# A two-layer decoder step in float32: the FFN's first products as seven half-size products, the second product as a phase of its own

## The chip, the core and the metric

The kernel runs on one core of one Trainium2 chip. TensorE (PE) multiplies, VectorE (DVE) and ScalarE (ACT) do the elementwise work, SyncE (SP) issues nearly all DMAs from one queue, in order. The metric is device time in microseconds: for before, the median of three runs.

## The reference, cut to what matters

One step of a two-layer model for 1,024 prompt tokens and 32 sample tokens, which the kernel handles as 1,056 columns side by side. Layer 0 mixes with gated linear attention, layer 1 with dilated attention. After each mixer stands the same feed-forward network (FFN), with 1,024 features and a hidden width of 2,816:

```python
def swiglu_ffn(x, g, w_in, w_out):
    a, b = jnp.split(rms_norm(x, g) @ w_in, 2, axis=-1)
    return (jax.nn.silu(a) * b) @ w_out
...
        x = x + h.astype(x.dtype)
        x = x + swiglu_ffn(x, f_norm[i], f_w_in[i], f_w_out[i]).astype(x.dtype)
        x = x + per_layer_embed(x, p[i], e_norm[i], e_w_proj[i], e_w_gate[i]).astype(x.dtype)
```

`w_in` has 5,632 output columns: 22 tiles of 128 for `a` and 22 for `b`. All is float32.

## The kernel before

Features lie on the 128 partitions, tokens along the free axis: the residual stream is eight tiles `X[0..7]` of 128x1056. A product in nearly full precision is made of three matmuls in the type fp32r. Each operand is split into a high part (ACT's copy into fp32r) and a low part (DVE's subtraction of the high part), and hi·hi, hi·lo and lo·hi are added up in PSUM. `split` does this for tokens (`XH`, `XL`, `GH`, `GL`), and `wtile` for a weight tile of 128 output columns, which it loads first (`raw`, then `whi`, `wlo`).

`proj` multiplies one weight tile with all tokens: per tile of 128 input features three products, each in three matmuls of 352 columns (`CW`), so 72 matmuls where there are eight tiles of features. The two PSUM pools `mma` and `mmb` take turns, each of three banks.

`block` runs once per layer, and is what the change rewrites. The output projection of the mixer goes in two halves of the features (`mix_out`, or the end of `mixer` for the first half in layer 1). As the second half adds to `X[m]`, `second` renormalizes this tile into `XH[m]`, `XL[m]` (the gain alone; the factor 1/rms of a token, `rstd`, is applied to the product later) and adds its squares to `ssq`. `norm_done` sums `ssq` over the partitions with small matmuls (`p_n`) and takes a root on ACT and a reciprocal on DVE in three pieces.

The FFN then runs over the hidden tiles in five chunks (`FCH`). For each hidden tile two projections with `w_fi` give `a` and `b`, and `silu(a)*b` is split into `GH`, `GL`. After a chunk, eight products with `w_fo`, one for each `X[m]`, add the chunk's share to the residual. First and second products so alternate, and everything between them stays in SBUF.

The order within each engine comes from a scheduler in the build: it interleaves instructions of different phases, but each engine and each queue then runs strictly in that order. SP's queue holds the weight loads as well as the stores and loads of activations: an entry that waits holds up all behind it.

## Time and profile before

| | |
|---|---|
| median of three runs | 3043.79 us (3042.93 to 3048.19) |
| span of the profiled execution, first to last instruction | 3039.0 us |
| PE busy / PE weight loads busy | 2997.8 us (99%) / 2874.2 us (95%) |
| DVE busy / ACT busy | 1468.7 us (48%) / 956.5 us (31%) |
| matmuls, each with a weight load of its own | 18,900 |
| share of the chain that ended last: PE | 91%, of it line 164 (`proj`) 73% |

The span is the kernel's own part of a run; the runs shown lie 3.9 to 9.2 us above it. "PE busy" counts any time in which at least one matmul is in flight, and matmuls overlap: the mean duration of one is longer than the distance between the starts of two.

### The profile page before, as it was taken

The numbers are of one execution on the slowest core, as the hardware profiler recorded it, in microseconds if no ns is written. First come the engines' busy times: TensorE is split into PE (matmuls) and PEld (weight loads), VectorE is DVE, ScalarE is ACT, GpSimd is POOL, SyncE is SP. The second block draws the span as 40 slices with busy tenths as digits, with TensorE's granted clock in tenths as the row PEclk, the third lists the DMA queues.
The fourth block names the chain that finished last, engine by engine and source line by source line (L and its number), as shares of the span: only waits on it lengthen the run. The fifth ranks groups of instructions, "written<-read, shape, count | busy, mean of one in ns | idle before, by whom it ended". The sixth has DMA issues, their size and how long they took to land.

```text
span 3039.0 us, 43739 instructions
## 1 busy us (share of the span) xinstructions
PE 2997.8 (99%) x18900; PEld 2874.2 (95%) x18900; DVE 1468.7 (48%) x2095; ACT 956.5 (31%) x1515; POOL 20.1 (1%) x44
## 2 busy tenths in 40 slices
...
GB/s 131 54 71 50 72 126 102 42 42 51 38 58 35 57 46 60 28 78 90 141 97 104 51 120 43 113 125 113 59 36 55 37 54 43 42 52 60 32 62 76
DMA packets 109776, 208.65 MB, mean 69 GB/s; under 512 B 31472, under 2 KB 54000, under 8 KB 108560
## 3 DMA queue, kind: packets, MB, share of 16 engines
...
## 4 chain that ended last, share of the span: by engine, by line
PE 91%; DVE 4%; DMA 3%; ACT 1%; issue 1%; SPq 0%; ACTq 0%
PE mm L164 73%; PE mm L712 6%; PE mm L182 1%; PE p_s L759 1%; PE p_o L827 1%; DMA vv<-in_cv_dram 1%; DVE q L586 1%; DVE hs L594 1%; DMA kk<-in_ck_dram 1%; DVE q L596 1%; DVE hs L595 1%; PE p_u L390 1%; PE p_us L408 1%; PE p_s L748 1%; PE p_o L399 1%
## 5 line engine op out<-in xcount | busy, mean ns | idle before, releaser
L164 PE MATMUL mm<-XH,whi 128*128 128x352 f32 x3312 | 728.5, 326 | 2.1 <-ACT whi L120 2.1
L164 PE MATMUL mm<-XL,whi 128*128 128x352 f32 x3312 | 723.5, 325 | 0.0
L120 ACT CAST whi<-raw 128x1024 fp32r<-128x1024 f32 (+4 forms) x288 | 247.5, 859 | 1507.4 <-PE mm L164 1430.9
L164 PE MATMUL mm<-XH,wlo 128*128 128x352 f32 x3312 | 716.9, 324 | 0.0
L164 PEld LDWEIGHTS mm<-XH,whi 128*128 128x128 f32 x3312 | 563.9, 188 | 11.3 <-issue 3.1
L164 PEld LDWEIGHTS mm<-XH,wlo 128*128 128x128 f32 x3312 | 566.1, 189 | 2.3 <-issue 1.6
L164 PEld LDWEIGHTS mm<-XL,whi 128*128 128x128 f32 x3312 | 564.1, 188 | 3.1 <-issue 1.6
L121 DVE TENSOR_TENSOR wlo<-raw,whi 128x1024 fp32r<-128x1024 f32 (+4 forms) x288 | 282.0, 979 | 15.5 <-ACT whi L120 15.2
L164 PE MATMUL mm<-GL,whi 128*128 128x352 f32 x1302 | 279.3, 322 | 0.0
L164 PE MATMUL mm<-GH,wlo 128*128 128x352 f32 x1302 | 279.2, 322 | 0.0
L164 PE MATMUL mm<-GH,whi 128*128 128x352 f32 x1302 | 278.5, 322 | 0.0
L537 DVE TENSOR_TENSOR X<-mm,X 128x1056 f32<-128x1056 f32 (+1 forms) x84 | 101.0, 1204 | 301.2 <-PE mm L164 301.0
L532 DVE TENSOR_TENSOR s<-mm,s 128x1056 f32<-128x1056 f32 x44 | 55.4, 1258 | 344.2 <-PE mm L164 344.2
L164 PEld LDWEIGHTS mm<-GL,whi 128*128 128x128 f32 x1302 | 220.9, 188 | 0.5 <-DVE GL L121 0.5
L164 PEld LDWEIGHTS mm<-GH,wlo 128*128 128x128 f32 x1302 | 220.8, 188 | 0.0
L164 PEld LDWEIGHTS mm<-GH,whi 128*128 128x128 f32 x1302 | 220.8, 188 | 0.0
L191 DVE TENSOR_TENSOR s<-mm,rstd 128x1056 f32<-128x1056 f32 x42 | 52.8, 1258 | 342.1 <-PE mm L164 342.1
L712 PE MATMUL mm<-XL,whi 128*128 128x352 f32 x576 | 193.5, 336 | 0.0
L712 PE MATMUL mm<-XH,whi 128*128 128x352 f32 x576 | 192.7, 334 | 0.0
L712 PE MATMUL mm<-XH,wlo 128*128 128x352 f32 x576 | 189.3, 329 | 0.0
L712 PEld LDWEIGHTS mm<-XH,whi 128*128 128x128 f32 x576 | 108.5, 188 | 3.7 <-issue 3.2
L712 PEld LDWEIGHTS mm<-XL,whi 128*128 128x128 f32 x576 | 108.6, 189 | 2.7 <-issue 1.2
...
## 6 DMA issues: line engine op xcount, KB each, us to landing
raw<-in_w_fi_dram SPq DMA_DIRECT2D x88, 512.0 KB, 3.2
...
raw<-in_w_a_dram SPq DMA_DIRECT2D x24, 512.0 KB, 3.3
raw<-in_w_q_dram SPq DMA_DIRECT2D x24, 512.0 KB, 3.4
kk<-in_ck_dram SPq DMA_DIRECT2D x40, 256.0 KB, 3.5
vv<-in_cv_dram SPq DMA_DIRECT2D x40, 256.0 KB, 2.9
raw<-in_w_eg_dram SPq DMA_DIRECT2D x16, 512.0 KB, 3.2
x<-in_x_t_dram SPq DMA_DIRECT2D x8, 528.0 KB, 9.2
```

The lines of the kernel that those rows point to most:

```text
L120: nc.scalar.copy(hi, x)
L121: nc.vector.tensor_tensor(lo, x, hi.bitcast(F32), op=ALU.subtract)
L164: nc.tensor.matmul(ps[:, c, :CW], a[:, k, :], b[k][:, c * CW:(c + 1) * CW], start=(k == 0 and i == 0), stop=(k == n - 1 and i == 2),)
L182: nc.tensor.matmul(ps, a[:, k, :], b[k][:, s], start=(k == 0 and i == 0), stop=(k == n - 1 and i == 2))
L191: nc.vector.tensor_tensor(v3(dst), ps, v3(rstd), op=ALU.mult)
L390: nc.tensor.matmul(p, kr[:, j], vt[:, j], start=True, stop=True)
L399: nc.tensor.matmul(po[:, i], vt[:, j, v], atts[j // 4][:, j % 4], start=True, stop=(j == 0))
L408: nc.tensor.matmul(p, kr[q, 8], vm[q], start=True, stop=True, tile_position=(16 * j, 0))
L532: nc.vector.tensor_tensor(v3(s), ps, v3(s), op=ALU.mult)
L537: nc.vector.tensor_tensor(like(X[m], s, p), p, like(X[m], s, p), op=ALU.add)
L586: nc.vector.scalar_tensor_tensor(dst[:, :NP].rearrange("p (r u) -> p u r", r=4)[:, u], q[:, :e].rearrange("p (u r) -> p u r", r=4), g, t[: ...
L712: nc.tensor.matmul(ps, a[:, k, :], b[k][:, s], start=(k == 0 and i == 0), stop=(k == n - 1 and i == 2))
```

## The change

For a hidden tile the two weight tiles (for `a` and `b`), each cut into two halves of the input features, form a 2x2 matrix of blocks, and the tokens, cut into two halves of 528 and the same two halves of features, form another. Such a 2x2 product needs eight block products; a Strassen-like (Winograd) form needs seven, and sums of blocks on both sides.

- `seven_tokens` makes the seven token operands once per layer for each pair of feature tiles `X[k]`, `X[k+4]`: four sums of 528 columns, and splits.
- `seven_weights` makes the seven weight operands for each hidden tile: four sums of 128x512, one split of 128x1024 and five of 128x512. Its tiles have one buffer each (`w7`), except `whi`, `wlo`.
- `one_of_seven` issues 24 matmuls of 264 columns (`HC`), so 168 per hidden tile where 144 of 352 stood. `gated` runs the products in the order 1, 6, 2, 7, 5, 4, 3 into three PSUM tiles (`al`, `be`, `ga`). Some continue to add to a PSUM tile after its interim value has been read. `u`, `v`, `s`, `g` take the results.
- `gated` stores each finished `g` to DRAM (`Gd`). When all 22 are done, a second phase loads them (`gr`), splits them and does the second products, in six chunks.
- The first half of the output projection goes to DRAM too (`Xp`) and is loaded again, as is the finished residual (`Xr`), since the token operands take the room.
- The second half of the output projection runs in the order m = 0, 4, 1, 5, 2, 6, 3, 7.

The diff, cut to its core:

```diff
--- before.py
+++ after.py
@@ -24,7 +24,9 @@
 NH = 22
 EPS = 1e-6
 SC = 128 ** -0.5
-FCH = [5, 5, 5, 4, 3]
+FCH = [4, 4, 4, 4, 3, 3]
+HT = T // 2
+HC = HT // 2
 AFTER = 2
 EP_AT = (3, 5, 6)
 QB = 4
...
     XH, XL = [], []
 
+    xh_pool = []
     def open_x():
...
 
     Xd = [dr.tile([128, T], F32, name=f"Xd{k}") for k in range(KT)]
+    Xp = [dr.tile([128, T], F32, name=f"Xp{k}") for k in range(KT)]
+    Xr = [dr.tile([128, T], F32, name=f"Xr{k}") for k in range(KT)]
...
+    def seven_weights(pool, src1, src2):
+        r1, r2 = (raws.tile([128, 1024], F32, tag="raw", name="raw") for _ in range(2))
+        nc.sync.dma_start(r1, src1)
+        nc.sync.dma_start(r2, src2)
+        a11, a12, a21, a22 = r1[:, :512], r1[:, 512:], r2[:, :512], r2[:, 512:]
+        s1, s2, s3, s4 = (pool.tile([128, 512], F32, tag=f"S{n}", name=f"S{n}") for n in range(1, 5))
+        def parts(n, x):
+            hi, lo = (pool.tile([128, 4, 128], F32R, tag=f"{a}{n}", name=f"{a}w") for a in "hl")
+            split(*(t[:].rearrange("p k m -> p (k m)") for t in (hi, lo)), x)
+            return hi[:], lo[:]
+        hi, lo = (wp.tile([128, 8, 128], F32R, tag=t, name=t) for t in ("whi", "wlo"))
+        split(*(t[:].rearrange("p k m -> p (k m)") for t in (hi, lo)), r1)
+        out = {1: (hi[:, :4], lo[:, :4]), 2: (hi[:, 4:], lo[:, 4:])}
+        nc.vector.tensor_tensor(s1, a21, a22, op=ALU.add)
+        nc.vector.tensor_tensor(s2, s1, a11, op=ALU.subtract)
+        out[6] = parts(6, s2)
+        nc.vector.tensor_tensor(s3, a11, a21, op=ALU.subtract)
+        out[7] = parts(7, s3)
+        out[5] = parts(5, s1)
+        out[4] = parts(4, a22)
+        nc.vector.tensor_tensor(s4, a12, s2, op=ALU.subtract)
+        out[3] = parts(3, s4)
+        return out
+    def seven_tokens(x1, x2, tiles, temp):
+        a, b = slice(0, HT), slice(HT, T)
+        t12, t34 = temp("t12"), temp("t34")
+        nc.vector.tensor_tensor(t12[:, a], x1[:, b], x1[:, a], op=ALU.subtract)
+        nc.vector.tensor_tensor(t12[:, b], x2[:, b], t12[:, a], op=ALU.subtract)
+        bo = tiles("B1")
+        split(bo[:, a], bo[:, b], x1[:, a])
+        out = {1: (bo[:, a], bo[:, b])}
+        nc.vector.tensor_tensor(t34[:, a], x2[:, b], x1[:, b], op=ALU.subtract)
+        nc.vector.tensor_tensor(t34[:, b], x2[:, a], t12[:, b], op=ALU.subtract)
+        for x, n1, n2 in ((t12, 5, 6), (x2, 2, 3), (t34, 7, 4)):
+            hi, lo = tiles("Bh"), tiles("Bl")
+            split(hi, lo, x)
+            out[n1], out[n2] = (hi[:, a], lo[:, a]), (hi[:, b], lo[:, b])
+        return out
+    def one_of_seven(n, ps, w, xs, first):
+        hi, lo = w[n]
+        for k, x in enumerate(xs):
+            xh, xl = x[n]
+            for i, (a, b) in enumerate(((hi, xh), (hi, xl), (lo, xh))):
+                for c in range(2):
+                    nc.tensor.matmul(ps[:, c, :HC], a[:, k, :], b[:, c * HC:(c + 1) * HC],
+                                     start=(first and k == 0 and i == 0), stop=(k == len(xs) - 1 and i == 2),
+                                     skip_group_check=not first)
+    def v2(ap):
...
-    def block(i, sx, src, w_o, gla_scope=None, X=None):
-        """X: the residual stream with the first half of the output projection"""
-        sg = ExitStack()
-        if X is None:
-            xp = sx.enter_context(tc.tile_pool(name="xp", bufs=1, side="right"))
-            X = [xp.tile([128, T], F32, name=f"X{k}") for k in range(KT)]
+    def gated(i, pool, X7, temp):
+        with ExitStack() as st:
+            pa, pb, pc = (psum(n, st, **k) for n, k in (("pa", {}), ("pb", {}), ("pc", dict(side="right"))))
+            a, b = slice(0, HT), slice(HT, T)
+            def pt(p, name):
+                return p.tile([128, 2, 512], F32, tag="pp", name=name)
+            def add(dst, ps, other):
+                nc.vector.tensor_tensor(v2(dst), ps[:, :, :HC], v2(other), op=ALU.add)
+            for j in range(NH):
+                w = seven_weights(pool, w_fi[i, j], w_fi[i, NH + j])
+                al, be, ga = pt(pa, "al"), pt(pb, "be"), pt(pc, "ga")
+                u, v, s, g = temp("u"), temp("v"), temp("s"), temp("g")
+                one_of_seven(1, al, w, X7, True)
+                nc.scalar.copy(v2(u[:, a]), al[:, :, :HC])
+                one_of_seven(6, be, w, X7, True)
+                add(u[:, b], be, u[:, a])
+                one_of_seven(2, al, w, X7, False)
+                nc.vector.tensor_tensor(v2(s[:, a]), al[:, :, :HC], v2(rstd[:, a]), op=ALU.mult)
+                one_of_seven(7, be, w, X7, False)
+                add(v[:, a], be, u[:, a])
+                one_of_seven(5, ga, w, X7, True)
+                add(g[:, b], ga, v[:, a])
+                one_of_seven(4, be, w, X7, False)
+                add(g[:, a], be, u[:, a])
+                one_of_seven(3, ga, w, X7, False)
+                add(s[:, b], ga, u[:, b])
+                nc.vector.tensor_tensor(s[:, b], s[:, b], rstd[:, b], op=ALU.mult)
+                nc.vector.tensor_tensor(g, g, rstd, op=ALU.mult)
+                nc.scalar.activation(s, s, AF.Silu)
+                nc.vector.tensor_tensor(g, g, s, op=ALU.mult)
+                nc.sync.dma_start(Gd[j], g)
+    def block(i, sx, src, w_o, gla_scope=None):
         def first(m, s, ps):
-            nc.sync.dma_start(X[m], x_t[m])
-            nc.vector.tensor_tensor(v3(X[m]), ps, v3(X[m]), op=ALU.add)
+            x = et("xf")
+            nc.sync.dma_start(x, x_t[m])
+            nc.vector.tensor_tensor(v3(x), ps, v3(x), op=ALU.add)
+            nc.sync.dma_start(Xp[m], x)
 
         if gla_scope is not None:
             st, et, rest = gla_scope
             mix_out(0, src, w_o, (XH, XL), et, first, (AFTER, rest))
             st.close()
+        xp = sx.enter_context(tc.tile_pool(name="xp", bufs=8, side="right"))
+        sb, sw = ExitStack(), ExitStack()
+        bg = sb.enter_context(tc.tile_pool(name="bg", bufs=12, side="right"))
+        w7 = sw.enter_context(tc.tile_pool(name="w7", bufs=1))
+        def xt(name):
+            return xp.tile([128, T], F32, tag="X", name=name)
+        def bt(name, dtype=F32):
+            return bg.tile([128, T], dtype, tag="b", name=name)
+        X = {}
+        ssq, X7 = bt("ssq"), {}
+        def second(m, s, p):
+            nc.vector.tensor_tensor(like(X[m], s, p), p, like(X[m], s, p), op=ALU.add)
+            if s.stop < T:
+                return
+            nc.sync.dma_start(Xr[m], X[m])
+            if m == 0:
+                nc.scalar.activation(ssq, X[m], AF.Square)
+            else:
+                t = bt("sq")
+                nc.scalar.activation(t, X[m], AF.Square)
+                nc.vector.tensor_tensor(ssq, ssq, t, op=ALU.add)
+            nc.scalar.activation(X[m], X[m], AF.Copy, scale=gcol(G_F[i] + m))
+            if m > 3:
+                k = m - 4
+                if k == 3:
+                    norm_done(ssq)
+                left = [7, 0, 7, 2][k]
+                def tile_(name):
+                    nonlocal left
+                    left -= 1
+                    return xtile(name) if left >= 0 else bt(name, F32R)
+                X7[k] = seven_tokens(X[k], X[m], tile_, xt if k else bt)
+        H_, L_ = ([xtile(f"O{a}{k}") for k in range(4)] for a in "HL")
+        for k in range(4):
+            t = xtile("ot", F32)
+            nc.sync.dma_start(t, src[4 + k])
+            split(H_[k], L_[k], t)
+        for m in range(KT):
+            X[m] = xt(f"X{m}")
+            nc.sync.dma_start(X[m], Xp[m])
+        for m in (0, 4, 1, 5, 2, 6, 3, 7):
+            for s, p in pieces(wtile(w_o[m][:, 512:], 4), H_, L_, m == 7):
+                second(m, s, p)
+        mma_stack.close()
+        mmb_stack.close()
+        gated(i, w7, [X7[k] for k in range(4)], xt)
+        sw.close()
+        mm.pools, mm.n = [psum("mma", mma_stack), psum("mmb", mmb_stack, side="right")], 0
         tp = sx.enter_context(tc.tile_pool(name="tp", bufs=1))
         ssq = tp.tile([128, T], F32, name="ssq")
-        gp = sg.enter_context(tc.tile_pool(name="gp", bufs=1))
-        GH = [gp.tile([128, T], F32R, name=f"GH{k}") for k in range(5)]
-        GL = [gp.tile([128, T], F32R, name=f"GL{k}") for k in range(5)]
 
         def tmp(name, tag="s", bufs=4):
             return tp.tile([128, T], F32, tag=tag, name=name, bufs=bufs)
 
-        def second(m, s, p):
-            nc.vector.tensor_tensor(like(X[m], s, p), p, like(X[m], s, p), op=ALU.add)
-            renorm(m, X[m], G_F[i], s)
-            if s.stop == T:
-                square_sum(ssq, X[m], m == 0, tp)
-        mix_out(1, src, w_o, (GH, GL), tmp, second)
-        norm_done(ssq)
-        # FFN
+        X = [xt(f"X{m}") for m in range(KT)]
         pe = {}
 
         def embed(m):
@@ -512,28 +666,29 @@
             pe[m] = tmp("pe")
             nc.scalar.copy(v3(pe[m]), ps)
 
-        pH, pL = (GH[3], GH[4]), (GL[3], GL[4])
         m0 = 0
         for n in FCH:
             last = m0 + n == NH
+            GH, GL = [], []
+            for a in range(n):
+                t = tmp("gr")
+                nc.sync.dma_start(t, Gd[m0 + a])
+                GH.append(bt("GH", F32R) if last else xtile("GH"))
+                GL.append(bt("GL", F32R) if last else xtile("GL"))
+                split(GH[a], GL[a], t)
+            if m0 == 0:
+                for m in range(KT):
+                    nc.sync.dma_start(X[m], Xr[m])
             if last:
+                new_x()
+                pH, pL = ([bt(a, F32R) for _ in range(2)] for a in ("pH", "pL"))
                 for k in range(2):
                     t = tmp("pt")
                     nc.sync.dma_start(t, p_t[i, k])
                     split(pH[k], pL[k], t)
-            for a in range(n):
-                early = m0 + a == 0
-                ps = proj(wtile(w_fi[i, m0 + a]), XH, XL)
-                s = tmp("s")
-                scaled(s, ps, early)
-                nc.scalar.activation(s, s, AF.Silu)
-                nc.vector.tensor_tensor(s, s, rstd, op=ALU.mult)
-                ps = proj(wtile(w_fi[i, NH + m0 + a]), XH, XL)
...
@@ -931,22 +1087,22 @@
                 if s < 7:
                     q = mx.queries(s + 1)
             xh_stack.close()
-            xp = sx.enter_context(tc.tile_pool(name="xp", bufs=1, side="right"))
-            X = [xp.tile([128, T], F32, name=f"X{k}") for k in range(KT)]
             hp = st.enter_context(tc.tile_pool(name="hp", bufs=1, side="right"))
             H_ = [hp.tile([128, T], F32R, name=f"OH{k}") for k in range(4)]
             L_ = [hp.tile([128, T], F32R, name=f"OL{k}") for k in range(4)]
             for k in range(4):
-                nc.sync.dma_start(X[4 + k], Ad[k])
-                split(H_[k], L_[k], X[4 + k])
+                t = hp.tile([128, T], F32, tag="ot", name="ot", bufs=4)
+                nc.sync.dma_start(t, Ad[k])
+                split(H_[k], L_[k], t)
             for m in range(KT):
-                nc.sync.dma_start(X[m], Xd[m])
+                x = hp.tile([128, T], F32, tag="xf", name="xf", bufs=4)
+                nc.sync.dma_start(x, Xd[m])
                 for c, ps in mx.proj(wtile(w_ob[m][:, :512], 4), H_, L_):
                     s = slice(c * CW, (c + 1) * CW)
-                    nc.vector.tensor_tensor(X[m][:, s], ps, X[m][:, s], op=ALU.add)
-        return sx, X
```

How the order on the engines moves, at three places. First DVE in layer 0, where the FFN begins. Before, from the last tiles of the output projection (`X_3264` and `X_3265` are `X[6]` and `X[7]`) to the first weight tile behind the reciprocals:

```order
L500 TENSOR_TENSOR X_3264<-mm,X_3264 128x1056
L121 TENSOR_TENSOR wlo<-raw,whi 128x1024
L500 TENSOR_TENSOR X_3265<-mm,X_3265 128x352
L124 SCALAR_TENSOR_TENSOR XL_141<-X_3264,gt,XH_133 128x1056
L138 TENSOR_TENSOR ssq<-ssq,sq 128x1056
L124 SCALAR_TENSOR_TENSOR XL_142<-X_3265,gt,XH_134 128x352
L500 TENSOR_TENSOR X_3265<-mm,X_3265 128x352 x2
L121 TENSOR_TENSOR wlo<-raw,whi 128x1024
L124 SCALAR_TENSOR_TENSOR XL_142<-X_3265,gt,XH_134 128x352 x2
L138 TENSOR_TENSOR ssq<-ssq,sq 128x1056
L146 RECIPROCAL rstd<-rstd 128x352 x3
L121 TENSOR_TENSOR wlo<-raw,whi 128x1024
```

After, at the end of the same stretch: the last weight splits of the first hidden tile ahead of the reciprocals, then the token operands of the last pair (`X_3758` is `X[7]`, `t_4229` and `t_4230` its sums, `Bl` the low parts), and at the end `u<-be`, the reading of product 6, for which product 7 waits:

```order
L134 TENSOR_TENSOR lw<-raw,hw 128x512
L221 RECIPROCAL rstd<-rstd 128x352 x3
L175 TENSOR_TENSOR t_4229<-X_3758,t_4229 128x528
L179 TENSOR_TENSOR t_4230<-X_3758,X_3750 128x528
L180 TENSOR_TENSOR t_4230<-X_3758,t_4229 128x528
L134 TENSOR_TENSOR lw<-S_4266,hw 128x512
L134 TENSOR_TENSOR Bl<-t_4229,Bh 128x1056
L134 TENSOR_TENSOR Bl<-X_3758,Bh 128x1056
L134 TENSOR_TENSOR Bl<-t_4230,Bh 128x1056
L134 TENSOR_TENSOR lw<-S_4267,hw 128x512
L166 TENSOR_TENSOR S_4268<-raw,S_4266 128x512
L562 TENSOR_TENSOR u<-be,u 128x528
```

The reciprocals had one weight split and the first results behind them; now the operands of the last pair stand behind them, and ahead of the rows shown (not printed here) three low splits of 1,056 columns, the last piece of `X[7]`, two operations of 528 columns, the last sum of squares and three weight sums.

Second, SP where the second half of layer 1's output projection begins (`Ad` is the attention's output, `w_ob` the weights). Before, with the weight loads of the half before ahead and behind:

```order
L915 DMA Ad_109<-os 128x32
L153 DMA raw<-in_w_ob_dram 128x512
L467 DMA ot<-Ad_106 128x1056
L467 DMA ot<-Ad_107 128x1056
L467 DMA ot<-Ad_108 128x1056
L153 DMA raw<-in_w_ob_dram 128x512
L467 DMA ot<-Ad_109 128x1056
```

After:

```order
L1103 DMA Xp_101<-xf 128x1056
L228 DMA raw<-in_w_ob_dram 128x512 x2
L641 DMA ot<-Ad_144 128x1056
L645 DMA X_19620<-Xp_101 128x1056
L641 DMA ot<-Ad_145 128x1056
L641 DMA ot<-Ad_146 128x1056
L641 DMA ot<-Ad_147 128x1056
```

The first `ot` load now stands behind the store of the last `Xp` tile, and the built program makes it wait for the landing of this store, since `ot` and `xf` share room. In layer 0 it is the first weight load (`w_oa`) of the second half that stands behind the last store of `Xp`; there all `w_oa` loads stood together before.

Third, SP where the first products of layer 0 end. Before, the loads of both products' weights alternate:

```order
L153 DMA raw<-in_w_oa_dram 128x512 x7
L153 DMA raw<-in_w_fi_dram 128x1024 x10
L153 DMA raw<-in_w_fo_dram 128x640 x8
L153 DMA raw<-in_w_fi_dram 128x1024 x10
L153 DMA raw<-in_w_fo_dram 128x640 x8
```

After, from the store of the last but one `g`:

```order
L586 DMA Gd_130<-g 128x1056
L228 DMA raw<-in_w_fo_dram 128x512
L681 DMA X_9181<-Xr_102 128x1056
L681 DMA X_9182<-Xr_103 128x1056
L681 DMA X_9183<-Xr_104 128x1056
L681 DMA X_9184<-Xr_105 128x1056
L675 DMA gr<-Gd_110 128x1056
L675 DMA gr<-Gd_111 128x1056
L586 DMA Gd_131<-g 128x1056
L675 DMA gr<-Gd_112 128x1056
L675 DMA gr<-Gd_113 128x1056
```

The built program makes the load `gr<-Gd_110` wait for the last matmul of the first products (its room is that of `w7`); the loads of `Gd_112` and `Gd_113` stand behind the store of the last `g`, `Gd_131`.

## Rows read from the trace of the kernel before

**Rows 1.** The page: span and busy time of the engines, and shares of the last chain.

```profile
span 3039.0 us, 43739 instructions
PE 2997.8 (99%) x18900; PEld 2874.2 (95%) x18900; DVE 1468.7 (48%) x2095; ACT 956.5 (31%) x1515; POOL 20.1 (1%) x44
...
PE 91%; DVE 4%; DMA 3%; ACT 1%; issue 1%; SPq 0%; ACTq 0%
```

**Rows 2.** The chain in order of time: start us, length us, what, how many instructions.

```profile
447.84 67.51 PE mm L164 x423
...
525.61 1.35 PE p_n L144 x4
527.87 765.62 PE mm L164 x4750
...
2079.05 23.10 PE mm L712 x144
2102.14 39.90 PE mm L164 x252
```

**Rows 3.** Busy time in a stretch inside layer 0's FFN, by engine, with counts.

```profile
540.00:740.00 200.00, 200.00 (x1241) 200.00 (x1240) 59.96 (x53) 31.45 (x32) 0.00 (x0) 1.00 0.14 45
```

**Rows 4.** Groups of PE by line and shape: busy us, mean ns of one.

```profile
L164 PE MATMUL mm<-XH,whi 128*128 128x352 f32 x3312 | 728.5, 326 | 2.1 <-ACT whi L120 2.1
...
L759 PE MATMUL p_s<-KB,q 128*128 128x256 f32 x128 | 36.6, 399 | 0.5 <-DVE stA L741 0.5
...
L759 PE MATMUL p_s<-KB,q 128*128 128x128 f32 x128 | 22.0, 285 | 0.6
```

**Rows 5.** Timeline of weight loads within attention: start us, length us, count.

```profile
1587.28 0.97 PEld L827 LDWEIGHTS p_o<-pta,VA 128*128 128x128 f32 x8
```

**Rows 6.** Groups of weight loads by line and shape.

```profile
L164 PEld LDWEIGHTS mm<-XH,wlo 128*128 128x128 f32 x3312 | 566.1, 189 | 2.3 <-issue 1.6
```

**Rows 7.** Groups of DVE by line and shape.

```profile
L121 DVE TENSOR_TENSOR wlo<-raw,whi 128x1024 fp32r<-128x1024 f32 x160 | 194.7, 1217 | 15.0 <-ACT whi L120 14.8
...
L121 DVE TENSOR_TENSOR GL<-s,GH 128x1056 fp32r<-128x1056 f32 x44 | 55.4, 1258 | 5.3 <-ACT GH L120 4.9
...
L146 DVE RECIPROCAL rstd<-rstd 128x352 f32<-128x352 f32 x18 | 40.6, 2314 | 7.4 <-ACT rstd L145 7.4
L121 DVE TENSOR_TENSOR wlo<-raw,whi 128x640 fp32r<-128x640 f32 x48 | 39.1, 815 | 0.0
...
L121 DVE TENSOR_TENSOR wlo<-raw,whi 128x512 fp32r<-128x512 f32 x48 | 32.7, 682 | 0.3 <-ACT whi L120 0.3
...
L946 DVE TENSOR_TENSOR X<-mm,X 128x352 f32<-128x352 f32 x24 | 12.5, 521 | 17.6 <-PE mm L712 17.5
```

**Rows 8.** Groups of ACT by line and shape.

```profile
L529 ACT ACTIVATE s<-s 128x1056 f32<-128x1056 f32 x44 | 47.9, 1089 | 33.0 <-DVE s L191 32.6 <-DVE s L189 0.4
L120 ACT CAST GH<-s 128x1056 fp32r<-128x1056 f32 x44 | 47.4, 1078 | 33.8 <-DVE s L532 33.8
...
L120 ACT CAST whi<-raw 128x512 fp32r<-128x512 f32 x48 | 29.9, 622 | 176.5 <-PE mm L164 127.9 <-issue 28.9 <-PE mm L712 19.6
```

**Rows 9.** DMA issues: count, KB each, median us from issue to landing.

```profile
raw<-in_w_fi_dram SPq DMA_DIRECT2D x88, 512.0 KB, 3.2
...
ot<-Od SPq DMA_DIRECT2D x8, 528.0 KB, 4.6
...
raw<-in_w_oa_dram SPq DMA_DIRECT2D x16, 256.0 KB, 2.7
...
Xd<-X SPq DMA_DIRECT2D x7, 528.0 KB, 3.1
...
ot<-Ad SPq DMA_DIRECT2D x4, 528.0 KB, 5.8
```

**Rows 10.** Busy time in two stretches of attention; the third column from the right is PEclk.

```profile
2018.00:2022.40 4.40, 2.38 (x10) 1.43 (x9) 4.33 (x12) 4.40 (x14) 0.00 (x0) 1.00 0.97 252
2022.40:2029.30 6.90, 4.36 (x14) 4.18 (x15) 5.57 (x8) 2.62 (x5) 1.18 (x1) 0.51 0.80 175
```

30 lines of the change are left out of this document (19 added, 11 removed).

## The prediction, made before the changed kernel ran

> **What bounds the kernel now.** First the page [rows 1]: PE is busy in 2997.8 of 3039.0 us, DVE in 48%, ACT in 31%, and PE makes up 91% of the chain that ended last. PE could still be waiting inside that time, so the chain in order of time comes next [rows 2]: in layer 0 it runs from 527.87 us through 4,750 matmuls of line 164 without a break. These are the whole FFN of a layer: 22 hidden tiles x 2 x 72 = 3,168 matmuls for the first products and 1,584 for the second. 765.62 us / 4,750 is 161.2 ns from start to start, and a stretch of its own agrees: 1,241 matmuls in 200 us [rows 3]. There DVE works 60 us of 200 and ACT 31. So the FFN goes at the matmuls' own pace, and the first products of both layers take 6,336 x 161.2 ns = 1021.4 us. A kernel with fewer columns gains only if PE keeps as gapless a queue; the view of the stretch says how much room the other engines have for that, and the order on SP and DVE where it ends.
>
> **What the change removes: columns.** Per hidden tile 168 matmuls of 264 columns replace 144 of 352, so 7,392 in all, with a weight load each. No row has an fp32r matmul of 264 columns, so its pace is bounded. Were it all proportional to columns, 161.2 x 264/352 = 120.9 ns. For a fixed part I compare two shapes of one line [rows 4]: from 128 to 256 columns a matmul of L759 grows from 285 to 399 ns; these are float32 in two passes, so 0.445 ns per column and pass. 88 columns fewer than 352 take off 39.2 ns: 122.0. The weight load sets a floor: eight in a row of the same 128x128 shape take 0.97 us [rows 5], which with 0.19 us for one [rows 6] is 0.111 us from start to start. 122 lies above that. I take 122 ns: 7,392 x 0.122 = 901.8 us, a gain of 119.6 us (127.7 at 120.9; 97.4 at 125, where the slope from float32 rows would not hold fully). The upper bound is the 161.2 of today, if the loads pace; that is a rival below.
>
> Rows 1 show the loads busy 95%, rows 5 that eight of them need 0.111 us each. A rule speaks against the change here: the Trainium skill ("Perfetto Trace Analysis", Identifying the Most-Contended Engine) judges TensorE by the busy share of its weight loads and not of its matmuls. With loads busy 95% [rows 1] that rule makes them the contended part, and 1,056 more of them at 161.2 ns would add 170.2 us, where the sum above takes 119.6 off. By the rows the long busy time in the FFN would be waiting rather than work; no row shows it for fp32r at 264 columns.
>
> **The loop of a hidden tile.** 168 x 0.122 = 20.5 us on PE. DVE does, with 0.70 us for 512 to 528 elements (0.682 at 512, 0.815 at 640 [rows 7]) and 1.26 for 1,056: seven results of 528, two of 1,056, four weight sums, five low parts of 512, one of 1,024 (1.22) = 16 x 0.70 + 2 x 1.26 + 1.22 = 14.9 us. ACT does some 5. Both fit. The tight place is product 7, which adds to `be` and waits until `u<-be` has read product 6: PE leaves 2.9 us (product 2) between them. From the end of product 3 of the tile before, DVE first does two results, one low part, four weight sums and `g*s` (1.26), about 6.2 us; product 6 ends at 5.9; `u<-be` is done at 6.9 and product 7 can start at 8.8. The sums need a weight tile whose load is issued after the low part of product 4's weights, some 1.3 us before the tile's start, and lands 3.2 us later [rows 9], at 1.9, where DVE reaches it at 2.1. It may be about 2 us late before PE waits. I take nothing for the loop.
>
> The FFN's second products keep their 3,168 matmuls; the loads of `g`, its splits (as before) and eight more additions of 1.26 us per layer lie beside them, where DVE had 140 of 200 us free.
>
> **What the change adds: six places where PE's queue runs dry.** Before, none of them has a gap: layer 0's halves of the projection run through (the run from 447.84 [rows 2]), layer 1's second half starts at 2102.14, as the first ends, and the FFN follows two norm pieces after the projection.
> - *Layer 0, second half of the projection.* Its first weights stand on SP behind the store of the last `Xp`. So: addition 1.26, load at 2.7 to 4.6 us (two big transfers go just ahead), cast 0.62: 4.6 to 6.5. Take 6.
> - *Layer 1, the same place.* The first `ot` load waits for that store to land: addition 0.52, store 3.1, load 4.6 to 5.8, cast 1.08 [rows 8, 9] = 9.3 to 10.5. Take 10.
> - *Start of the FFN, both layers.* DVE must work off its list between the last projection matmul and `u<-be` of the first hidden tile, in this order: weight split 1.22, three low parts 3.77, the last piece of `X[7]` 0.52, two operations of 528 1.4, squares 1.26, five weight operations 3.5, three reciprocals 6.94, three sums 2.1, one weight part 0.7, three low parts 3.77, two weight operations 1.4, `u<-be` 0.7 = 27.3 us. PE has four products to do meanwhile, 96 x 0.122 = 11.7, and six norm matmuls, about 2 (1.35 for four). It loses 13.6; the pairs before load DVE almost as fully, so I take 14 (11 to 18) per layer, 28.
> - *From first to second products, both layers.* The first `gr` load waits for the last matmul; it lands after 3.2 (512 KB of weights) to 4.6 us (`ot<-Od`), say 4, and its cast takes 1.08. The third load stands behind the last store of `g`, ready after two results, the silu and a product, 0.7 + 0.7 + 1.09 + 1.26 = 3.75. It lands at 7.75; cast 8.8; low parts of the third and fourth tile at 10.1 and 11.4; the rest of the first second product 1. So 12.4 where 36 x 0.161 = 5.8 is PE's own work: 6.6; take 7 (5.8 to 9), 14 in all.
> - *The clock.* After a stretch in which PE worked 2.4 of 4.4 us, the granted clock was 0.51 for 6.9 us [rows 10], about 3.5 us lost. Six pauses of 6 to 14 us may each cost something like it, in part within the pause: take 5 in all (0 to 20).
>
> **The sum.** -119.6 + 6 + 10 + 28 + 14 + 5 = -56.6 us. On the profiled span of 3039.0 us that is 2982.4; the median of the runs lies 4.8 us above that span, which I leave as it is: 2987 us. With the ends of the terms: -127.7 + 4.6 + 9.3 + 22 + 11.6 = -80 (2964), and -97.4 + 6.5 + 10.5 + 36 + 18 + 20 = -6 (3037).
>
> **The rivals.**
> - *The pauses are mostly covered.* If DVE's list overlaps better than in order of the rows, and loads land early, some 30 us are lost instead of 63: 3043.8 - 119.6 + 30 = 2954. Against it: the order is fixed in the program, and its reciprocals are real [rows 7].
> - *The loads pace the matmuls.* At 161.2 ns unchanged: +170.2 + 63 = 3277 us. It decides from 7,392 x p = 1021.4 - 63, so p = 129.7 ns, on. For it: the 189 ns of one load [rows 6] is longer than 122. Against it: rows 5. That is the case in which the rule above would be right.
> - *The loop waits for its second weight tile.* If its load lands beyond the 2 us of room, each further microsecond costs 43: from 1.3 us on the change is slower, at 3 us 3116. For it: one buffer each for the raw tiles, and 3.2 us is a median [rows 9]. Against it: no other transfer is due there.
> - *The pauses cost twice what I take*, with half clock behind each: 3043.8 - 119.6 + 126 = 3050.
> - *A lower pace per matmul.* At the floor of the loads, 0.111 us [rows 5], the gain would be 200.9 us, and the time 2906. Against it: 264 columns would then go much faster, each, than 352 do in 161.2 ns [rows 3]. The Trainium skill ("TensorE: Matmul & The Clock Gate", Back-to-back issue gap) has such a rule, columns/2.4 + 2.5 ns: an estimate of 112.5 ns at 264, a gain of 190 us and 2917 us by it; the trace disagrees at 352 columns, where the rule has 149.2 ns.
>
> That the change does not do what it says is no rival: the order shows 168 matmuls of 264 columns per hidden tile.
>
> **How the numbers follow.** Chances: forecast (2964 to 3037) 0.70; pauses covered 0.10; lower pace 0.03; loads pace 0.05; loop waits 0.06; pauses twice 0.06. About 0.2% (6 us) is what a measurement here can tell from no change. Faster: 0.69 of the forecast's 0.70, both cases below it, and 0.04 of loop and pauses: 0.86. Same: 0.04. Slower: 0.10. The range runs from 2945, below which only the lower pace lies, to 3040, just above the forecast's upper end; it leaves out some 0.15.
>
> **What would show it.** The mean of a matmul's start-to-start in the first products: about 1,640 in 200 us if 122 ns holds; 1,240 if the loads pace. PE waiting for DVE (`lw`, `Bl`, `u`) at each start of an FFN, some 14 us; for ACT's cast of `GH` between the phases, with a DMA just before; for `OH` in layer 1 about 10, for `whi` in layer 0 about 6. Gaps that come back 22 times per layer would be the loop. I would be wrong above all if the pace lies far from 122 ns, or if the pauses sum to half or double 63.

## The result, and the profile after

The changed kernel takes 3000.19 us (median of 4 runs, 2996.83 to 3001.56) where the kernel before takes 3043.36 us (4 runs, 3040.59 to 3048.19). The ratio is 0.9856, with a 95% interval from 0.9842 to 0.9870: 43.2 us, or 1.4%, faster. The prediction said 2987 us in a range of 2945 to 3040, and faster with a chance of 0.86. The median lies 13 us above the forecast.

The page of the changed kernel, with the same lines as [rows 1]:

```profile
span 2998.7 us, 47341 instructions
PE 2902.7 (97%) x19956; PEld 2770.8 (92%) x19956; DVE 1866.5 (62%) x2787; ACT 1095.9 (37%) x1777; POOL 20.3 (1%) x44
...
PE 85%; DVE 8%; DMA 3%; ACT 2%; issue 1%; SPq 0%; DVEq 0%; ACTq 0%
```

PE is no longer busy all the time: DVE now makes up 8% of the chain where it made up 4%, and DMA still 3%. Where the pauses lie is seen by cutting both traces at the same places of the program. First the kernel before, stage by stage (columns: stretch, its length, busy us and count of PE, weight loads, DVE, ACT, POOL; granted clock; DMA share; GB/s). The cuts are the end of the first half of the output projection, the end of its second half, the end of the FFN, and the same for layer 1:

```profile
0.00:475.28 475.28, 465.47 (x2810) 413.95 (x2811) 243.54 (x273) 181.30 (x249) 2.75 (x12) 1.00 0.25 90
475.28:520.92 45.64, 45.64 (x290) 45.64 (x289) 32.27 (x31) 20.69 (x23) 0.00 (x0) 1.00 0.19 64
520.92:1297.84 776.92, 776.92 (x4815) 775.65 (x4814) 266.47 (x241) 147.67 (x160) 0.00 (x0) 1.00 0.15 47
1297.84:2101.98 804.14, 778.24 (x5219) 709.64 (x5218) 578.20 (x1232) 406.05 (x866) 17.31 (x32) 0.99 0.32 99
2101.98:2147.62 45.64, 45.64 (x290) 45.64 (x289) 31.60 (x31) 20.97 (x23) 0.00 (x0) 1.00 0.20 64
2147.62:2924.32 776.70, 776.70 (x4815) 775.66 (x4814) 266.48 (x241) 149.00 (x161) 0.00 (x0) 1.00 0.15 47
2924.32:3039.00 114.68, 109.20 (x672) 108.05 (x671) 50.12 (x50) 30.78 (x36) 0.00 (x0) 0.99 0.20 72
```

The same view of the changed kernel, with one cut more in each FFN, between first and second products. Behind them are a stretch inside the first products and three short ones that are read further down:

```profile
0.00:475.07 475.07, 466.02 (x2810) 413.83 (x2810) 241.48 (x271) 179.09 (x246) 2.75 (x12) 1.00 0.28 101
475.07:538.94 63.87, 50.85 (x290) 50.15 (x289) 40.97 (x47) 30.68 (x35) 0.00 (x0) 0.89 0.43 151
538.94:1005.80 466.86, 457.38 (x3703) 454.96 (x3702) 322.33 (x433) 135.44 (x188) 0.00 (x0) 0.99 0.24 81
1005.80:1277.14 271.34, 265.94 (x1643) 265.20 (x1641) 136.09 (x140) 73.86 (x94) 0.00 (x0) 0.99 0.32 103
1277.14:2076.18 799.04, 777.66 (x5218) 708.87 (x5217) 572.63 (x1227) 401.20 (x861) 17.55 (x32) 1.00 0.34 105
2076.18:2145.34 69.16, 51.95 (x291) 49.76 (x289) 45.04 (x50) 35.13 (x38) 0.00 (x0) 0.88 0.43 153
2145.34:2612.80 467.46, 457.74 (x3704) 454.85 (x3702) 321.89 (x433) 136.23 (x189) 0.00 (x0) 0.99 0.24 81
2612.80:2884.26 271.46, 266.15 (x1643) 265.43 (x1642) 135.89 (x140) 73.62 (x94) 0.00 (x0) 0.99 0.33 103
2884.26:2998.70 114.44, 108.95 (x673) 107.77 (x671) 50.20 (x50) 30.67 (x36) 0.00 (x0) 1.00 0.20 72
...
600.00:800.00 200.00, 200.00 (x1642) 200.00 (x1640) 134.79 (x185) 55.15 (x77) 0.00 (x0) 1.00 0.23 78
485.00:490.00 5.00, 5.00 (x21) 5.00 (x20) 0.69 (x1) 0.62 (x1) 0.00 (x0) 0.58 0.30 108
560.00:565.00 5.00, 5.00 (x28) 5.00 (x27) 4.68 (x7) 0.62 (x1) 0.00 (x0) 0.58 0.23 64
565.00:570.00 5.00, 5.00 (x44) 5.00 (x43) 3.10 (x5) 2.92 (x4) 0.00 (x0) 1.00 0.10 41
```

The second row of each fence is the same 288 matmuls of layer 0: 45.64 us before, 63.87 after; in layer 1 they take 45.64 and 69.16. In 200 us of first products stand 1,642 matmuls, 121.8 ns each, where [rows 3] has 1,241. With these rows the sum of the prediction can be checked term by term (us, against the kernel before; "predicted" is the prediction's own term; 3,696 are the first products of one layer, 1,638 the 1,584 second products with 54 of the embedding that stand among them):

| term | predicted | measured | from the rows |
|---|---|---|---|
| pace of 7,392 matmuls, at 122 ns | -119.6 | -119.6 | 1,642 in 200 us; 122 ns kept |
| layer 0, second half of the projection | +6 | +18.2 | 63.87 - 45.64 |
| layer 1, the same place | +10 | +23.5 | 69.16 - 45.64 |
| start of the FFN, layers 0 and 1 | +14, +14 | +14.0, +14.6 | 466.86 and 467.46, less 3,696 x 0.122 + 2.0 of the norm |
| first to second products, both layers | +14 | +14.7 | 271.34 + 271.46, less 2 x 1,638 x 0.1612 |
| half clock, wherever it falls | +5 | in the four terms above | |
| all the rest | 0 | -5.5 | rows 1, 4, 7 of before against rows 1, 5, 9 |
| sum | -56.6 | -40.1 | spans: 2998.7 - 3039.0 = -40.3 |

So on the span the prediction missed 16 us, and nearly 26 us of misses stand in one place: the second half of the projection, whose 16 us came out as 41.7. In the time it missed only 13, because it carried over the 4.8 us by which the median of before lies above its profiled span; in the changed kernel these are 1.5. The waits of PE say what is late there (engine, line, who is waited for: us, times, longest):

```profile
PE mm L239 <- ACT OH L133: 12.5, 1, 12.5
PE mm L239 <- ACT GH L133: 10.7, 4, 4.9
PE mm L239 <- ACT whi L133: 8.9, 1, 8.9
...
PE be L194 <- DVE lw L134: 5.9, 1, 5.9
PE mm L239 <- DVE wlo L134: 4.7, 3, 2.9
PE al L194 <- DVE Bl L134: 3.5, 1, 3.5
...
PE mm L239 <- DVE X L614: 2.7, 3, 1.2
```

`OH` is layer 1's entry (the start of the projection's second half), `whi` layer 0's, `GH` the boundary from first to second products in both layers, `lw` and `Bl` the starts of the FFN in layers 0 and 1: five of the six that the prediction named; there is no wait for `u`. Two it did not name, `wlo` and `X`, stand behind the entries.

The chain in order of time at the two entries, layer 0 and layer 1 (start, length, what):

```profile
477.44 5.91 DMA raw<-in_w_oa_dram
...
483.43 0.63 ACT whi L133
...
2082.01 0.70 DVE wlo L134
2083.16 4.50 DMA ot<-Ad
2087.72 1.08 ACT OH L133
```

In layer 0 the first weights are issued 2.4 us after the first half ended at 475.07 (the prediction had an addition of 1.26 us ahead of them; a store and a reload stand on SP too), and take 5.9 us to land, where the prediction had 2.7 to 4.6. What is under way beside them are the store of `Xp[7]`, issued at 476.55, and reloads of `Xp`; the `ot` load issued at 471.13 has landed by then, after 5.4 us.

In layer 1 the prediction had the right chain and one length wrong: the store of `Xp[7]`, for whose landing the first `ot` load waits, takes 5.7 us where the prediction had 3.1. Its issue on SP, and the time to landing of this one store:

```profile
2076.93 0.32 SPq L1103 DMA_DIRECT2D Xp<-xf  x1
...
DMA to landing us min/median/max: 5.7/5.7/5.7
```

It lands at 2082.6. Ahead of the `ot` load on SP stands a raw weight load as well, which waits for the split `wlo` (2082.01 to 2082.71) to free its buffer; so either of the two would have held the `ot` load, which goes out at 2083.16, to about 2082.7.

Behind the entries DVE's part of the same chain shows why `X` and `wlo` are late, here in layer 0:

```profile
509.34 1.25 DVE Bl L134
510.59 1.17 DVE X L614
511.76 1.17 DVE Bl L134
...
515.33 0.61 DVE wlo L134
```

The addition `X`, which frees a PSUM tile, and the next weights' low part `wlo` stand in DVE's list among and behind the token operands of the first pair (`Bl` is three of them); DVE works without a gap from 503.98 to 515.9, more than half of it on token operands. From the distances of matmul starts, of the 9.2 and 10.9 us that PE loses behind the entries (the column "rest" below) 4.5 and 5.5 are waits, and 4.2 and 4.7 are matmuls at half clock, 0.29 us apart where 0.16 is usual.

### The profile page after: what moved, and what is told of

Read it like the earlier page. It is cut to its first block, busy times and chain, and to the rows that moved or that the text cites. A ratio compares the mean times of both kernels' runs of the same rounds, so it can differ in the third digit from the quotient of the medians.

```text
span 2998.7 us, 47341 instructions
## 1 busy us (share of the span) xinstructions
PE 2902.7 (97%) x19956; PEld 2770.8 (92%) x19956; DVE 1866.5 (62%) x2787; ACT 1095.9 (37%) x1777; POOL 20.3 (1%) x44
## 4 chain that ended last, share of the span: by engine, by line
PE 85%; DVE 8%; DMA 3%; ACT 2%; issue 1%; SPq 0%; DVEq 0%; ACTq 0%
PE mm L239 39%; PE be L194 12%; PE ga L194 8%; PE al L194 8%; PE mm L869 6%; PE p_s L916 1%; PE mm L257 1%; PE p_o L984 1%; DVE q L741 1%; DVE hs L749 1%; DVE hs L750 1%; DVE q L751 1%; DVE Bl L134 1%; PE p_u L467 1%; PE p_us L485 1%
## 5 line engine op out<-in xcount | busy, mean ns | idle before, releaser
L134 DVE TENSOR_TENSOR wlo<-raw,whi 128x1024 fp32r<-128x1024 f32 (+3 forms) x260 | 231.2, 890 | 75.4 <-ACT whi L133 75.2
L239 PE MATMUL mm<-XH,whi 128*128 128x352 f32 x1200 | 271.3, 331 | 0.4 <-ACT q_in L263 0.4
L239 PE MATMUL mm<-XL,whi 128*128 128x352 f32 x1200 | 265.4, 327 | 0.0
L239 PE MATMUL mm<-XH,wlo 128*128 128x352 f32 x1200 | 264.0, 326 | 0.0
L194 PE MATMUL be<-Bh,lw 128*128 128x264 f32 x1056 | 216.2, 286 | 5.9 <-DVE lw L134 5.9
L194 PE MATMUL be<-Bh,hw 128*128 128x264 f32 x1056 | 216.4, 286 | 1.8 <-ACT hw L133 1.7
L194 PE MATMUL be<-Bl,hw 128*128 128x264 f32 x1056 | 216.7, 287 | 0.0
L239 PEld LDWEIGHTS mm<-XH,whi 128*128 128x128 f32 x1200 | 205.3, 189 | 9.1 <-issue 2.5
L239 PEld LDWEIGHTS mm<-XL,whi 128*128 128x128 f32 x1200 | 205.3, 189 | 3.2 <-issue 1.3
L239 PEld LDWEIGHTS mm<-XH,wlo 128*128 128x128 f32 x1200 | 204.1, 189 | 2.2 <-issue 1.6
L869 PE MATMUL mm<-XL,whi 128*128 128x352 f32 x576 | 193.6, 336 | 0.0
L869 PE MATMUL mm<-XH,whi 128*128 128x352 f32 x576 | 193.2, 335 | 0.0
L869 PE MATMUL mm<-XH,wlo 128*128 128x352 f32 x576 | 188.9, 328 | 0.0
```

Of the source, the lines that this page charges most:

```text
L134: nc.vector.tensor_tensor(lo, x, hi.bitcast(F32), op=ALU.subtract)
L194: nc.tensor.matmul(ps[:, c, :HC], a[:, k, :], b[:, c * HC:(c + 1) * HC], start=(first and k == 0 and i == 0), stop=(k == len(xs) - 1 and i ...
L239: nc.tensor.matmul(ps[:, c, :CW], a[:, k, :], b[k][:, c * CW:(c + 1) * CW], start=(k == 0 and i == 0), stop=(k == n - 1 and i == 2),)
L869: nc.tensor.matmul(ps, a[:, k, :], b[k][:, s], start=(k == 0 and i == 0), stop=(k == n - 1 and i == 2))
```

## The experiments

Each was run beside the kernel before on the same chip (medians of before from 3041.5 to 3044.4 us). The table gives, for the profiled execution of each, where PE lost time, from the start times of its matmuls in the trace. *Entry*: from the end of the projection's first half to the first matmul of its second. *Rest*: from there to the end of its 288 matmuls, less their 45.6 us of before. *First products*: their stretch less 3,696 x 0.122 + 2.0. *Second products*: their stretch whole, from the last first product on. *Between*: from there, in layer 0, to the end of the first half of layer 1's projection (804.1 before).

| kernel | span | entry, layers 0 / 1 | rest | first products | second products | between |
|---|---|---|---|---|---|---|
| the change | 2998.7 | 9.0 / 12.7 | 9.2 / 10.9 | 14.1 / 14.6 | 271.1 / 271.2 | 799.2 |
| late_recip | 2989.9 | 9.1 / 12.8 | 8.1 / 10.0 | 12.3 / 7.9 | 270.8 / 270.9 | 801.8 |
| early_gr | 2984.4 | 9.0 / 12.4 | 9.5 / 10.0 | 13.0 / 14.2 | 263.5 / 263.4 | 803.8 |
| late_x | 2985.2 | 0.0 / 10.1 | 6.8 / 8.1 | 12.8 / 14.4 | 271.0 / 271.1 | 804.9 |
| one_pair | 2954.5 | 8.8 / 12.6 | 4.4 / 5.6 | -0.7 / -1.7 | 271.0 / 271.0 | 797.6 |
| three_edits | 2957.9 | 0.0 / 9.5 | 7.4 / 7.3 | 12.0 / 5.9 | 263.5 / 263.4 | 802.2 |
| four_edits | 2954.6 | 0.0 / 6.8 | 7.4 / 9.5 | 11.9 / 7.5 | 263.4 / 263.5 | 797.0 |
| five_edits | 2956.5 | 0.0 / 6.5 | 7.7 / 10.8 | 11.5 / 8.5 | 263.5 / 263.5 | 798.6 |
| norm_later | 2947.1 | 0.0 / 6.4 | 6.8 / 10.2 | 6.4 / 5.5 | 263.5 / 263.5 | 798.7 |
| tile_twice | 2996.8 | 9.5 / 11.5 | 8.6 / 12.0 | 15.8 / 14.2 | 271.0 / 270.5 | 797.5 |

The last column differs by 8 us between executions, though no edit is aimed at that stretch. So the -5.5 us of "all the rest" above need no cause in the change, and single edits are judged by their own columns, not by the span. A column is still one execution: in kernels whose edit is aimed elsewhere, an entry scatters by up to 1.3 us, a rest by up to 2.0, a start by up to 1.3.

**late_recip: the reciprocals out of the list.**

```diff
-    def norm_done(ssq, n=D):
+    def norm_done(ssq, n=D, invert=True):
...
                 add(u[:, b], be, u[:, a])
+                if j == 0:
+                    invert()
                 one_of_seven(2, al, w, X7, False)
...
-                    norm_done(ssq)
+                    norm_done(ssq, invert=False)
```

`invert` issues the three reciprocals of `rstd`.

> The three reciprocals of the norm are issued after the sum that reads product 6 of the first hidden tile, instead of ahead of the token and weight operands. Theory of the prediction (VectorE works off a list in order, and the reciprocals' 6.94 us stand in it ahead of what PE waits for): the loss at the start of each FFN (13.5 and 14.9 us) falls by about 7 us per layer, with a little of the half clock on top, so 13 to 17 us less in all. Rival (the list is not what PE waits for, but the landing of the second raw weight tile or the token operands behind it): under 4 us less. Rival 2 (the reciprocals only move, and PE waits for them at product 4's tile a little later): half of it, 6 to 8 us.

Measured: 2994.85 us (2989.35 to 2998.32), ratio to the kernel before 0.9841 (0.9821 to 0.9862). The start lost 1.8 us less in layer 0, which is little above the scatter, and 6.7 in layer 1: 8.5 in all, where the theory had 13 to 17 and the second rival 6 to 8. DVE's timeline of the change shows the list in layer 0 (start, length, line):

```profile
548.89 6.77 DVE L221 RECIPROCAL rstd<-rstd 128x352 f32<-128x352 f32 x3
...
562.92 0.71 DVE L562 TENSOR_TENSOR u<-be,u 128x528 f32<-128x528 f32 x1
```

The projection's last matmul ends at 538.94, and DVE works without a gap from there to `u<-be`, which ends 24.7 us later; the prediction's list was 27.3 us. In late_recip `u<-be` starts at 555.37, 17.9 us after its projection ended where the change has 24.0, but the reciprocals then delay `s<-al`, which frees the tile of the next product, and a new wait of PE stands there:

```profile
PE al L194 <- DVE s L581: 4.1, 1, 4.1
```

So the second rival holds in layer 0, where the 6.94 us were mostly pushed to the next wait; in layer 1 they were saved, as the theory had it.

**early_gr: the loads of the second phase ahead.**

```diff
+                if j == NH - 1:
+                    ahead()
...
+        def ahead():
+            for a in range(FCH[0]):
+                t = xt("gr")
+                nc.sync.dma_start(t, Gd[a])
+                early.append(t)
...
```

> The first four loads of g for the second phase go into tiles of the pool of u, v, s, g and are issued ahead of the last store of g, so that they wait neither for the last matmul of the first phase nor for that store. Theory of the prediction: the loss between the phases (7.3 us in each layer) falls to under 1 us, 12 to 14 us less in all. Rival (another thing is late at the boundary, the first weights of the second product or the casts on ScalarE): half or less, under 7 us.

Measured: 2987.85 us (2983.44 to 2991.34), 0.9816 (0.9801 to 0.9832). The second phase takes 263.5 us instead of 271.1 in each layer, and no wait is left ahead of it: 15.4 us in all (the theory had 12 to 14), the prediction's term with what half clock follows it. So it was the late loads alone that made the boundary.

**late_x: the reloads with their products.**

```diff
-        for m in range(KT):
+        turn = (0, 4, 1, 5, 2, 6, 3, 7)
+        def again(m):
             X[m] = xt(f"X{m}")
             nc.sync.dma_start(X[m], Xp[m])
-        for m in (0, 4, 1, 5, 2, 6, 3, 7):
+        for n, m in enumerate(turn):
+            again(m)
```

> The reload of the half-finished residual X[m] is issued with its own product m, not all eight ahead of the second half of the projection. Theory (in layer 0 the first weights stand behind stores and reloads on SP and share the DMA engines with three big transfers; in layer 1 the wait is for the ot load): the pause at the entry of layer 0 falls from 9.0 to about 3 us, that of layer 1 stays within 2 us of 12.7; the rest of the second half (9.2 and 10.8 us over the kernel before) stays, 5 to 8 us less in all. Rival (the rest of the second half is waiting for these reloads and for transfers, not for VectorE): the rest falls to 4 us in each layer too, 16 to 20 us less in all.

Measured: 2984.59 us (2983.82 to 2987.03), 0.9808 (0.9793 to 0.9823). Layer 0's entry is gone, better than expected: the first weights are now issued ahead of the last stores. Layer 1's fell by 2.6 us, where it was to stay. The rest fell by 2.4 and 2.8 us, not to 4, so that reloads and transfers are not what most of it waits for; in layer 0 the matmul starts show why it fell at all: its waits are the same 4.5 us, and the 2.4 us at half clock behind the entry are gone with the entry's pause. The span is 13.5 us shorter, between the theory's 5 to 8 and the rival's 16 to 20.

**one_pair: without three quarters of the token operands.**

```diff
-                X7[k] = seven_tokens(X[k], X[m], tile_, xt if k else bt)
+                X7[k] = seven_tokens(X[k], X[m], tile_, xt if k else bt) if k == 0 else X7[0]
```

> The seven token operands are made for the first pair of feature tiles only, and serve all four pairs (the products of the other three pairs are left out of the result); matmuls and weights are as before. Theory: what the second half of the projection loses after its entry (9.2 us in layer 0, 10.8 in layer 1), and the start of the FFN, is VectorE's work on the token operands, which stands in order ahead of the additions that free PE's PSUM tiles. Then the rest of the second half falls to 3 to 5 us (half clock after the entry alone), and the loss at the FFN's start from 14 to 3 to 5 us, in each layer. Rival (that rest is half clock and transfers, the FFN's start hangs on weight tiles and reciprocals): the rest stays over 8 us, the start over 10.

Measured: 2956.29 us, one run. The windows of layer 0's second half and first products:

```profile
474.55:533.43 58.88, 48.62 (x290) 48.07 (x291) 33.35 (x37) 26.93 (x31) 0.00 (x0) 0.94 0.45 162
533.43:985.60 452.17, 452.13 (x3702) 451.09 (x3700) 309.90 (x419) 128.83 (x180) 0.00 (x0) 1.00 0.23 83
```

The loss at the start is gone: 452.17 us, with PE busy 452.13, though the reciprocals still stand ahead of `u<-be` in DVE's list. The rest of the projection's second half falls to 4.4 and 5.6 us. So the work on the token operands of three pairs is the start's loss, and 4.8 and 5.3 us of the rest. The edit takes away ACT's casts of these operands too; that the part of DVE is what counts is read from the waits, not shown by a run. What remains of the rest in layer 0:

```profile
PE mm L239 <- DVE X L614: 1.2, 1, 1.2
PE mm L239 <- DVE wlo L134: 0.5, 1, 0.5
```

These are waits behind the operands of the first pair, which the edit keeps. By the matmul starts, 2.0 of the 4.4 us left are such waits and 1.8 half clock; in layer 1 it is 2.5 and 2.5 of 5.6.

**three_edits, four_edits, five_edits: together, and one step on each time.** three_edits is late_x and early_gr, and the first piece below, for the FFN's norm alone; four_edits adds the second piece, and five_edits puts the four sums of `seven_tokens` on GpSimd (one of them shown):

```diff
+            if on_act:
+                nc.scalar.activation(rstd[:, s], p, AF.Ln, scale=1.0 / n, bias=epsb)
+                continue
             nc.scalar.activation(rstd[:, s], p, AF.Sqrt, scale=1.0 / n, bias=epsb)
             nc.vector.reciprocal(rstd[:, s], rstd[:, s])
+        if on_act:
+            nc.scalar.activation(rstd, rstd, AF.Exp, scale=-0.5)
...
-            t = xtile("ot", F32)
+            t = bt("ot") if i else xtile("ot", F32)
...
-        nc.vector.tensor_tensor(t12[:, a], x1[:, b], x1[:, a], op=ALU.subtract)
+        nc.gpsimd.tensor_tensor(t12[:, a], x1[:, b], x1[:, a], op=ALU.subtract)
...
```

> late_x and early_gr together, and the reciprocal root of the FFN's norm made on ScalarE by a logarithm and an exponential, so that VectorE has no reciprocals there at all. Theory (VectorE's list is what PE waits for at the FFN's start, and late_recip only pushed 6.94 us behind the next wait): the start loses 6 to 8 us per layer where it lost 13 to 15; with 13.5 us from late_x and 14.3 from early_gr the profiled span is 2998.7 - 13.5 - 14.3 - 14 = 2957 us. Rival (ScalarE becomes late, with its table loads and the casts queued behind, or the savings overlap): 2966 us or more.

> three_edits, and in layer 1 the four ot loads of the second half go into another pool, whose room does not wait for the last store of the first half. Theory (the entry of layer 1 waits for these loads alone): its pause falls from about 10 us to 1 to 3, 7 to 10 us less than three_edits, 2948 us. Rival (the operands' room itself, or the first weights, come next): its pause stays over 5 us, 0 to 5 us less.

> four_edits, and the four sums of 528 columns of each pair's token operands on GpSimd, 2.8 us a pair off VectorE. No row shows GpSimd's price for such a sum. Theory (VectorE's token work is the bound after the entry): 3 to 8 us less than four_edits, provided that GpSimd takes less than 3 us a sum. Rival (GpSimd is far slower, or slows VectorE meanwhile): as four_edits or up to 15 us more, with PE waiting for Bh, whose sums are late.

Measured: 2959.23 us (2954.86 to 2959.67), 2957.40 (2955.55 to 2959.66) and 2958.70 (2957.16 to 2959.74); ratios 0.9723 (0.9708 to 0.9737), 0.9722 (0.9706 to 0.9738) and 0.9724 (0.9710 to 0.9739). three_edits came out at 2957.9 us of span against the 2957 expected, but not by the split expected: layer 0's start still loses 12.0 us. There `u<-al`, a copy on ACT, is late, behind the table load and the logarithm. four_edits shows that wait, and why layer 1's entry fell by less than half of what was expected (the second line is ACT's own wait, in layer 1):

```profile
PE al L194 <- ACT u L576: 3.5, 1, 3.5
...
ACT OH L133 <- DMA Xp<-xf: 3.0, 1, 3.0
```

The loads are early now, but the cast writes its operand into room that the last store still reads: the rival was right. With GpSimd nothing changes that can be told: a sum took 1.3 to 2.2 us there in the trace where DVE takes 0.70, and the first products lost no less (20.0 us in both layers against 19.4). The rival stands.

**norm_later: the norm behind product 6.** four_edits, and in the first hidden tile:

```diff
                 add(u[:, b], be, u[:, a])
+                if j == 0:
+                    norm()
```

`norm` issues the six matmuls, the logarithm and the exponential.

> four_edits, and the whole norm of the FFN (PE's six matmuls too) issued after the sum that reads product 6 of the first hidden tile, so that neither its table loads nor its logarithm stand on ScalarE ahead of the copy of product 1. Theory (with VectorE's list shorter, ScalarE's copy u<-al is what PE waits for, 3.5 us in layer 0): the loss at the start falls from 11.9 and 8.1 us to about 7 each, 5 to 7 us less than four_edits. Rival (what is left is VectorE's token operands alone): within 2 us of four_edits.

Measured: 2947.04 us (5 runs, 2945.46 to 2950.64), ratio 0.9683 (0.9669 to 0.9696); the change has 0.9856. The start loses 6.4 and 5.5 us, 7.5 less in all than in four_edits, whose interval of the ratio (0.9706 to 0.9738) lies wholly above. It is the fastest kernel of this study with the whole computation, 3.2% below the kernel before where the change is 1.4% below. What it still pays is 6.4 us at layer 1's entry, 17.0 in the rest and 11.9 at the starts.

**tile_twice: is the loop close to waiting?**

```diff
         nc.sync.dma_start(r2, src2)
+        nc.sync.dma_start(r2, src2)
```

> The changed kernel, with the second raw weight tile of each hidden tile loaded twice, one load after the other, so that it lands about 3.5 us later. By the prediction's rival of the waiting loop (2 us of room, then 44 us for each microsecond): 1.5 us in each of 44 hidden tiles, about 64 us more, 3064 us. If the loop has more room than the prediction worked out: under 20 us more. If VectorE, late, is not caught up by the next tile either: over 100 us more.

Measured: 2998.60 us, one run: no slower than the change. DVE waits for the tile in every hidden tile (ten of them between 700 and 905 us, 1.3 us each), where in the change it waits 0.9 us in two of ten; PE waits once, for 0.7 us, in more than 400 us:

```profile
DVE S L160 <- DMA raw<-in_w_fi_dram: 13.0, 10, 3.1
...
PE be L195 <- DVE u L563: 0.7, 1, 0.7
```

But the order of DVE's list was not the same in this kernel: the sums that need the tile stand behind `g*s`, and `u<-be` ahead of two of the four. The traces are aligned by the sum `g<-be`, which waits for PE in both (818.73 in the change, 819.98 here): the first sum of the tile then starts 3.4 us later, and `u<-be` only 0.6 us later (808.87 less 1.25, against 807.07). So a tile 3.4 us late costs nothing once the list gives way. What it would cost in the change's own order is not shown.

**cols176, no_pause176, mid176: the pace, and the clock.** In the first of these each matmul but the first two of a product takes 176 columns instead of 264, as below; the second adds late_x and one_pair; the third has such narrow matmuls in hidden tiles 8 to 13 alone:

```diff
-                    nc.tensor.matmul(ps[:, c, :HC], a[:, k, :], b[:, c * HC:(c + 1) * HC],
+                    w_ = HC if k == 0 and i == 0 else 176
+                    nc.tensor.matmul(ps[:, c, :w_], a[:, k, :], b[:, c * HC:c * HC + w_],
```

> Only the size of the disputed cost: in every one of the seven products each matmul but the very first of an accumulation takes 176 columns of each 264 (a third of the sums is left out of the products). 7,392 matmuls and weight loads stay. If columns alone set the pace (0.445 ns per column, as the prediction had it), a matmul inside a product takes 122.0 - 39.2 = 83 ns from start to start, and the loop of a hidden tile is then held by VectorE at 14 to 15 us. If the weight loads have a floor near the one the prediction took (0.111 us), it takes about 111 ns and the loop about 18.7 us. If the loads had paced the changed kernel all along, 122 ns and 20.5 us as now.

> late_x, one_pair and cols176 together: matmuls of 176 columns (a third of the sums left out), operands of one pair for all, and no pause of PE ahead of the first hidden tile of layer 0. In cols176 the granted clock stood at 0.50 through both first phases, after the pauses at their start. If a pause lets the clock fall and the narrow matmuls only fail to bring it back, layer 0's first phase now runs at 1.00 and about 107 ns a matmul (213 ns at half clock), some 395 us. If the stream of narrow matmuls itself brings it down, its clock is 0.50 with no pause before, and the phase takes some 790 us again.

> The changed kernel, with matmuls of 176 columns (the last third of each sum left out, but for the first matmul of an accumulation) in hidden tiles 8 to 13 of each layer alone, in the middle of the first products, where PE has no pause for 400 us. no_pause176 still had waits of PE ahead of the fall of the clock; here there are none. If only a pause lets the clock fall: it stays at 1.00, a matmul takes 111 ns, those six hidden tiles take 112 us instead of 123, and the kernel about 22 us less than 2998.7. If the stream of narrow matmuls lowers it by itself: 0.50 in those tiles, 213 ns a matmul, some 215 us, and about 185 us more in all, if the clock comes back as soon as the matmuls are wide again.

Measured, one run each: 3668.84, 3619.52 and 3133.34 us. None had expected the first. With narrow matmuls the granted clock is 0.50, the lower of its two levels, through nearly all of both layers' first products: 213 ns from start to start. no_pause176 has the same, but it still had waits of 2.3 and 3.4 us ahead of the fall. In mid176 the fall can be read in the middle of the phase; its stretches, with the columns as above:

```profile
719.00:742.70 23.70, 23.70 (x214) 23.70 (x213) 16.39 (x24) 5.95 (x9) 0.00 (x0) 1.00 0.24 83
742.70:746.00 3.30, 1.08 (x10) 0.92 (x9) 2.75 (x5) 2.09 (x3) 0.00 (x0) 1.00 0.22 56
746.00:764.10 18.10, 18.10 (x163) 18.10 (x163) 10.92 (x17) 3.54 (x5) 0.00 (x0) 1.00 0.22 79
764.10:767.60 3.50, 1.09 (x10) 0.92 (x9) 2.95 (x5) 2.09 (x3) 0.00 (x0) 1.00 0.16 51
767.60:772.00 4.40, 4.40 (x24) 4.40 (x23) 1.76 (x3) 1.00 (x1) 0.00 (x0) 0.53 0.50 201
772.00:900.70 128.70, 128.70 (x604) 128.70 (x604) 49.29 (x69) 19.98 (x29) 0.00 (x0) 0.50 0.12 42
900.70:902.00 1.30, 1.30 (x11) 1.30 (x11) 1.30 (x3) 0.00 (x0) 0.00 (x0) 0.90 0.00 0
```

Two things follow. At full clock 163 matmuls, nearly all narrow, take 18.10 us, 111.0 ns each: the floor of the loads that the prediction took from [rows 5], and not the 83 ns of columns alone. And the clock: narrow matmuls ran at 1.00 for 45 us, through one wait of PE of 2.2 us (the second row); after another wait, of 2.4 us, it fell to 0.50 and stayed there for 130 us without a gap; it was back about 1.4 us after the matmuls were 264 columns wide again, in tile 14. In layer 1 it fell after the first wait, of 2.1 us. So each fall seen here stands behind a wait of PE, and the rise behind the first wide matmuls. Neither of the two theories had that whole: the first had the fall, the second the price. Whether narrow matmuls without any wait would keep 1.00 is not shown, since no run has them so for longer than 24 us.

## Why the prediction was right, and where it was not

- **The whole**: the time lies in the range, and the kernel is faster, as forecast. Part of the nearness is luck: the 5.5 us of "all the rest" and the 3.3 us by which the medians' distances from the spans differ (4.8 and 1.5) brought the time nearer to the forecast, and neither has a cause in its terms.
- **The pace** was right: 122.0 ns forecast, 121.8 measured, though no row showed that shape. No row showed the "two passes" either by which the prediction halved its slope from float32 matmuls; between 352 and 264 columns the slope is 39.4 ns for 88 columns, 0.448 per column against the 0.445 used, so it held. "The loads pace the matmuls" (3277 us) is out: 1,642 matmuls stand in 200 us where the loads are busy for all 200. The Trainium skill ("Perfetto Trace Analysis", Identifying the Most-Contended Engine) judges how near TensorE is to its limit by the busy share of its weight loads and by the share of peak arithmetic (MFU); that the loads then set the pace is a conclusion of the prediction, which goes further than the page. Here the loads are busy 200 of 200 us at 161.2 ns a matmul and at 121.8, so their busy share did not tell the pace; only in mid176, with fewer columns, is the pace that of the loads. "A lower pace" is out too: the floor of 111 ns is real, but reached only at 176 columns. The rule columns/2.4 + 2.5 ns, which the Trainium skill ("TensorE: Matmul & The Clock Gate", Back-to-back issue gap) gives for a matmul by itself, makes 112.5 ns at 264 columns, and the trace lies 9 ns above it. For pairs of weight load and matmul, which this kernel has, the same section of the Trainium skill names about 81 ns at 128 columns and 131 at 512; the trace disagrees with that as well, with 161.2 ns at 352.
- **The loop** was right: no wait of PE in over 400 us of first products. The rival's price of 43 us for each microsecond of lateness was not seen: in tile_twice 3.4 us cost nothing, with other work moved ahead of the late tile.
- **The FFN's start** was right in its cause, and in size in part by luck: 14.0 and 14.6 us against 14 each, gone when the token operands go (one_pair). DVE's list took 24.7 us where the prediction had 27.3, and by the matmul starts some 3.4 of the 14.0 us are half clock, which the prediction held in another term. That moving the reciprocals does not save their 6.94 us in layer 0 (late_recip) shows that there the list as a whole was the limit, not an item in it; in layer 1 moving them did save 6.7.
- **The boundary** was right: 14.7 against 14, and early_gr takes all of it away.
- **The second half of the projection** is the step that failed: "Take 6" and "Take 10" against 18.2 and 23.5. The entries themselves were under-sized by 3.0 and 2.7 us: in layer 0 the first weights land in 5.9 us beside the store and reloads of `Xp`, and in layer 1 the store of `Xp[7]` takes 5.7 us to land and not 3.1. The larger part, 9.2 and 10.9 us, was not in these terms at all. The prediction had written that "the pairs before load DVE almost as fully", and used it for the FFN's start alone; but DVE's token work already holds up the additions and weight parts that the projection needs (`wlo`, `X` in the waits). Three of the four pairs account for 4.8 and 5.3 us by one_pair; what is left is waits behind the first pair, and half clock.
- **The clock** was under-sized too: by the matmul starts, matmuls at half clock take some 18 us more than at full clock in the six places (9 in the two rests, 6 to 7 at the FFN's starts, 3 at the boundaries), where the prediction took 5 in a range to 20. It is contained in the measured terms above, in part beneath waits that would have been there anyway.
- **"Pauses are mostly covered"** (2954 us) and **"pauses twice"** (3050 us) are out: the pauses with their half clock sum to 85 us (the six terms of the table), where the forecast has 63 + 5 and the two rivals 30 and 126.

What stays open: what DVE and ACT each contribute to what one_pair saved, and whether the room of layer 1's operands could be had without the last store; neither was tried.
